# Chunks of 256 tokens as three passes of 256 columns, with both weight tiles shifted alike

## The chip, the cores and the metric

The kernel runs on one core of one Trainium2 chip. The metric is the device time of one execution in microseconds (us), as the median of several. Durations inside an execution come from one profiled execution, whose own time and span are given below.

## What is computed

One layer of a hybrid decoder trunk over 16 meta tokens and 256 sequence tokens (L = 272) with a model width of 2048. In the reference, cut to what matters here:

```
hn = rmsnorm(h_res, norm_g[l])                       # (272, 2048)
p = hn @ w_in[l]                                     # 176 blocks of 128 columns
glu_a, glu_b, conv_gate, q, k, v, ret_gate, merge_a, merge_b = ...  # slices of p
y_a = conformer_branch(...)      # glu, 31-tap conv, layernorm, * silu(conv_gate), @ conv_out
o = retention_chunkwise(q, k, v) # 8 heads
o = head_groupnorm(o, ...)
y_b = (o * silu(ret_gate)) @ ret_out[l]
merged = sigmoid(merge_a) * y_a + sigmoid(merge_b) * y_b
h_res = h_res + merged @ w_out[l]
return rmsnorm(h_res, final_norm_g)[:, 16:]
```

All inputs and outputs are float32. The output has 256 rows, so the parts that only scale or gate an output token (conv_gate, q, ret_gate, merge_a, merge_b) need the 256 sequence tokens alone, and the parts that feed the convolution or the keys and values need all 272.

## The kernel before

**Splitting.** TensorE multiplies in a float32r type. To keep float32 accuracy each operand is split into a high part and the rest (`split`, lines 52 to 54: a copy on ACT, a subtraction on DVE), and a product is the sum of three: high weights times high activations, high weights times low activations, low weights times high activations. The low-times-low product is left out.

**Chunks.** The program is one list `seq` of 240 weight chunks of 128 x 2048 floats (1 MB). Chunk i is loaded on the SP queue into `raw` (three buffers), split into a pair `whi` and `wlo` (three buffers each), and then used by TensorE. The engines run in the order in which the program issues to them; TensorE works chunk by chunk. 176 chunks are blocks of `w_in`, 32 of `ret_out`, 16 of `conv_out` and 16 of `w_out`.

**The activations.** `hn` holds the normalized tokens, transposed: 128 channels on the partitions, `[8, 2, 2, ROW]` behind it, that is block k mod 8, high or low, block k div 8, and a row of 288 floats of which 272 are used. `hn_row(k, low)` is a row of 272; `hn_wide(k)` is the high and the low row of block k without the 16 meta tokens, a pattern of 2 x 256.

**Two ways to multiply a chunk.** A chunk for all 272 tokens goes through `project` (lines 272 to 280): for each of 16 blocks k, high weights times the high row and high weights times the low row (lines 277 and 278), and then 16 times low weights times the high row (line 280). That is 48 matmuls of 272 columns into one PSUM row. A chunk for 256 tokens goes through `project_wide` (lines 282 to 289): high weights times both rows at once, 16 matmuls of 512 columns that fill two halves of a PSUM bank (line 289), and 16 matmuls of 256 columns with the low weights into the first half (line 288). The latter stand ahead of the last of the former. `halves` (lines 291 to 295) adds the two halves: ACT copies the second to SBUF (line 294), DVE adds the first (line 295). 96 chunks of `w_in` are of this kind (q, ret_gate, merge_b, conv_gate and merge_a), and the 16 of `conv_out`, whose activations are `fin["s"]`, written `s`.

**A third user of 256 columns** is `contract` (lines 297 to 304), for `ret_out`: three passes of 256 columns, high-high and high-low in turn (301, 302) and then low-high (304), with the tiles `zhi` and `zlo`. A chunk has 48 of these, and there are four chunks for each of the eight heads.

**Addresses.** Where the weights lie against the moving rows is set by hand in places. `halved` cuts a weight tile into two halves of 1024 floats, 1056 floats apart; the rows of blocks k and k + 8 in `hn` are 288 floats apart. Both distances are 128 bytes modulo 256, so that a block and its row keep one distance in both halves. The argument `first` of `stream` (16 for chunks of 256 tokens) shifts the low weights by 16 floats, 64 bytes, as the rows without the meta tokens start 16 floats further. The high weights are not shifted. By the addresses in the built program, the weight block that is loaded while a row streams lies 64 bytes (modulo 256) from that row in `project`, in `contract` and in the low passes of `project_wide`, and 0 bytes from it in most of the wide matmuls. At the step from block 7 to block 8 it is 128 bytes more, once in each pass over a halved tile.

The order of the 240 chunks: for each head sig_b and glu blocks, q and k, the four `ret_out` chunks of the head before, v, and the four ret_gate blocks; then 8 of merge_b, the last head's `ret_out`, 8 of merge_b, 16 of conv_gate, merge_a and `conv_out` in turn, and `w_out`.

Of the kernel before, what the change touches and what calls it, by code (L numbers as in the profile page):

```python
# [10 lines left out]
F32 = mybir.dt.float32  # L11
F32R = mybir.dt.float32r
AF = mybir.ActivationFunctionType
ALU = mybir.AluOpType
PSUM = bass.MemoryType.PSUM

P = 128
D = 2048
KT = D // P
# [20 lines left out]
def hybrid_kernel(ctx: ExitStack, tc, xt, xrow, xnat, par, fg, cs, dec, win, cout, rout, wout, out):  # L40
# [34 lines left out]
        return t[:, first:first + 2 * HALF_W].rearrange("p (h c) -> p h c", h=2)[:, :, 0:D // 2]  # L75

    def split_tiles(apart, first):
        hi = stage.tile([P, 2 * HALF_W], F32R, tag="whi", name="whi", bufs=SPLITS)
        lo = stage.tile([P, 2 * HALF_W + 64], F32R, tag="wlo", name="wlo", bufs=SPLITS)
        if not apart:  # L80
            return hi[:, 0:D], lo[:, first:first + D]
        return halved(hi), halved(lo, first)

    def block(w, k):
        return w[:, k * P:(k + 1) * P] if len(w.shape) == 2 else w[:, k // 8, k % 8 * P:(k % 8 + 1) * P]
# [193 lines left out]
        for k in ks:  # L279
            nc.tensor.matmul(acc[:, 0:L], lhsT=block(lo, k), rhs=hn_row(k, 0), start=False, stop=(k == KT - 1))  # L280

    def project_wide(acc, hi, lo, a):

        both = acc.rearrange("p (h t) -> p h t", h=2)
        for k in range(KT):
            if k == KT - 1:
                for j in range(KT):
                    nc.tensor.matmul(acc[:, 0:SEQ], lhsT=block(lo, j), rhs=a(j)[:, 0], start=False, stop=False)  # L288
            nc.tensor.matmul(both, lhsT=block(hi, k), rhs=a(k), start=(k == 0), stop=(k == KT - 1))  # L289

    def halves(acc, out):

        t = tmp.tile([P, SEQ], F32, tag="half", name="half")
        nc.scalar.copy(out=t, in_=acc[:, SEQ:])  # L294
        nc.vector.tensor_tensor(out=out, in0=acc[:, 0:SEQ], in1=t, op=ALU.add)

    def contract(acc, hi, lo, a_hi, a_lo, kts, col):

# [10 lines left out]
    def proj_chunk(blk, n, evac):  # L309
        def use(hi, lo, acc=None):  # L310
            if acc is not None:
                return lambda: evac(acc)
            acc = bank(misc if 4 <= seen[0] <= HELD else accp)
            seen[0] += 1
            if n == L:
                project(acc, hi, lo)
            else:
                project_wide(acc, hi, lo, hn_wide)
            return lambda: evac(acc)
        stream(win[blk], use, True, 0 if n == L else 16)  # L320

# [22 lines left out]
    def head(h):  # L344
# [20 lines left out]
        def rot(which, j, n):  # L365
            def f(acc):
                t = ret.tile([P, 2, n], F32, tag=f"rt{j}", name=f"rt{j}")
                s[which, j] = t
                if n == SEQ:
                    x = tmp.tile([P, SEQ], F32, tag="sg", name="sg")  # L370
                    halves(acc, x)
                    acc = x
                nc.vector.tensor_tensor(out=t, in0=acc[:, 0:n].unsqueeze(1).broadcast_to([P, 2, n]),
                                        in1=cs_sb[:, :, L - n:], op=ALU.mult)
                if j == 1:
                    t0, t1 = s[which, 0], t
                    r = ret.tile([P, 2, n], F32, tag=which + "r", name=which + "r")
                    nc.vector.tensor_tensor(out=r[:, 0], in0=t0[:, 0], in1=t1[:, 1], op=ALU.subtract)
                    nc.vector.tensor_tensor(out=r[:, 1], in0=t1[:, 0], in1=t0[:, 1], op=ALU.add)
                    hi = ret.tile([P, 2, n], F32R, tag=which + "hi", name=which + "hi")  # L380
                    lo = ret.tile([P, 2, n], F32R, tag=which + "lo", name=which + "lo")
                    split(r, hi, lo)
                    s[which] = (r, hi, lo)
            return f
# [8 lines left out]
        def gate(j):  # L393
            def f(acc):
                if j == 0:
                    s["g"] = ret.tile([P, 4 * SEQ + 16], F32, tag="gs", name="gs")[:, 0:4 * SEQ].rearrange(
                        "p (b t) -> p b t", b=4)
                g, t = s["g"][:, j], tmp.tile([P, SEQ], F32, tag="sg", name="sg")
                halves(acc, g)
                nc.vector.tensor_tensor(out=g, in0=g, in1=row[:, NMETA:], op=ALU.mult)  # L400
                nc.scalar.activation(out=t, in_=g, func=AF.Sigmoid)
                nc.vector.tensor_tensor(out=g, in0=g, in1=t, op=ALU.mult)
            return f
# [182 lines left out]
    fin = {}  # L586

    def sig_of(acc, t):
        halves(acc, t)
        nc.vector.tensor_tensor(out=t, in0=t, in1=row[:, NMETA:], op=ALU.mult)  # L590
        nc.scalar.activation(out=t, in_=t, func=AF.Sigmoid)

    def merge_b(d):
# [60 lines left out]
    def conv_gate(b):  # L654
        def f(acc):
            fp = fin["pool"]
            g = u_sb[b % 2][:, 0:SEQ]
            halves(acc, g)
            nc.vector.tensor_tensor(out=g, in0=g, in1=row[:, NMETA:], op=ALU.mult)
            t = tmp.tile([P, SEQ], F32, tag="sg", name="sg")  # L660
            nc.scalar.activation(out=t, in_=g, func=AF.Sigmoid)
            nc.vector.tensor_tensor(out=g, in0=g, in1=t, op=ALU.mult)
# [17 lines left out]
    def conv_out_use(d):  # L680
        def use(hi, lo):
# [1 line left out]
                fin["m"] = [pool.tile([P, NB, SEQ], F32R, tag=tag, name=f"m{i}")  # L683
                            for i, (pool, tag) in enumerate(((pers, "cm"), (fin["pool"], "m1")))]
            acc = bank(accp)
            project_wide(acc, hi, lo, lambda k: fin["s"][:, k])
            t = fin["ma", d]
            y = fin["pool"].tile([P, SEQ], F32, tag="lny", name="ya", bufs=2)
            halves(acc, y)
            nc.vector.tensor_tensor(out=t, in0=y, in1=t, op=ALU.mult)  # L690
            nc.vector.tensor_tensor(out=yb[:, d], in0=yb[:, d], in1=t, op=ALU.add)
            split(yb[:, d], fin["m"][0][:, d], fin["m"][1][:, d])
        return use
# [230 lines left out]
```

## Time and profile before

| what | value |
|---|---|
| median of 3 runs | 1415.52 us (1415.43 to 1416.01) |
| the profiled execution | 1416.04 us |
| its span, first to last instruction | 1414.3 us |
| PE busy with matmuls | 1404.7 us, 99% of the span |
| DVE, ACT busy | 1090.0 us, 691.4 us |
| bytes moved | 274.70 MB, 194 GB/s |

The span is what the trace shows; the execution's own time has 1.7 us around it. The profiled execution took 0.5 us more than the median. Matmuls overlap in the trace: one lasts longer than the time to the start of the next, so the pace is read from start to start, and the ends are modelled.

### The profile page before, as it was taken

Reading aid. Unit: us, or ns where it says so; the run is one execution under the profiler, and the core shown is the slowest. Engines: PE = TensorE matmul, PEld = TensorE weight load, DVE = VectorE, ACT = ScalarE, POOL = GpSimd, SP = SyncE. Lnnn points to the kernel's source line nnn. Section 1 sums busy time; section 2 is a strip of 40 time slices with the busy share of each in tenths; the row PEclk is TensorE's granted clock in tenths of the full one; section 3 lists DMA queues with packets and bytes.
Section 4 is the critical chain, followed back from the end, with each engine's and each line's share of the span. In section 5 each row is a group of like instructions: output and inputs, shape, how many; then the busy total and the mean of one; then the engine's idle time right before and its main releaser. Section 6 shows DMA issues by size and latency. Waiting matters only on the chain.

```text
span 1414.3 us, 23358 instructions
## 1 busy us (share of the span) xinstructions
PE 1404.7 (99%) x9648; PEld 1311.4 (93%) x9648; DVE 1090.0 (77%) x1513; ACT 691.4 (49%) x823; POOL 176.1 (12%) x317
## 2 busy tenths in 40 slices
PE   9999999999999999999999999999999999999997
PEld 9999999999999999999999999989988888888887
DVE  6799957986895797698689579976688876666553
ACT  6554635445544534544553454355356654444432
POOL 0032023003203201400320320032000000000000
PEclk9999999999999999999999999999999999999999
DMA  9665556556555655665555565566555555555752
GB/s 327 247 210 185 179 193 200 186 187 207 180 186 188 202 178 186 192 201 179 177 193 201 180 199 174 178 197 196 196 184 183 179 205 183 190 197 181 296 184 85
DMA packets 49467, 274.70 MB, mean 194 GB/s; under 512 B 9136, under 2 KB 9904, under 8 KB 18480
## 3 DMA queue, kind: packets, MB, share of 16 engines
q1 hardware_dynamic: 38352, 258.43, 53.1%
q0 software_dynamic: 9280, 8.93, 3.3%
q10 hardware_dynamic: 1728, 5.83, 1.2%
q8 instruction: 76, 1.25, 0.4%
q14 instruction: 31, 0.25, 0.0%
HBM read 262.15 MB, written 2.10 MB: 187 GB/s over the span
## 4 chain that ended last, share of the span: by engine, by line
PE 95%; DVE 2%; ACT 1%; DMA 1%; issue 1%; POOL 0%; POOLq 0%; DVEq 0%; ACTq 0%
PE ps L289 27%; PE ps L288 14%; PE ps L278 11%; PE ps L280 11%; PE ps L277 11%; PE ps L302 4%; PE ps L301 4%; PE ps L304 4%; PE ps L703 2%; PE ps L702 2%; PE ps L706 2%; DVE wlo L54 1%; DMA vy<-vx 0%; ACT whi L53 0%; PE ps L515 0%
## 5 line engine op out<-in xcount | busy, mean ns | idle before, releaser
L54 DVE TENSOR_TENSOR wlo<-raw,whi 128x2048 fp32r<-128x2048 f32 (+2 forms) x246 | 547.2, 2226 | 147.0 <-ACT whi L53 121.9
L53 ACT ACTIVATE whi<-raw 128x2048 fp32r<-128x2048 f32 (+2 forms) x246 | 459.6, 1870 | 270.0 <-PE ps L278 138.7
L289 PE MATMUL ps<-hn,whi 128*128 128x512 f32 x1536 | 374.7, 392 | 0.0
L289 PEld LDWEIGHTS ps<-hn,whi 128*128 128x128 f32 x1536 | 283.1, 188 | 55.7
L277 PE MATMUL ps<-hn,whi 128*128 128x272 f32 x1264 | 317.1, 287 | 0.0
L278 PE MATMUL ps<-hn,whi 128*128 128x272 f32 x1264 | 316.7, 287 | 0.0
L278 PEld LDWEIGHTS ps<-hn,whi 128*128 128x128 f32 x1264 | 238.2, 188 | 1.1
L277 PEld LDWEIGHTS ps<-hn,whi 128*128 128x128 f32 x1264 | 238.2, 188 | 0.3
L339 DVE SCALAR_TENSOR_TENSOR c_sb<-u,par_sb,c_sb 128x256 f32<-128x256 f32 x480 | 206.6, 476 | 1.5
L288 PEld LDWEIGHTS ps<-hn,wlo 128*128 128x128 f32 x1536 | 194.2, 189 | 7.6 <-DVE wlo L54 0.3
L288 PE MATMUL ps<-hn,wlo 128*128 128x256 f32 x1536 | 195.8, 280 | 0.0
L280 PE MATMUL ps<-hn,wlo 128*128 128x272 f32 x1264 | 171.1, 287 | 0.0
L280 PEld LDWEIGHTS ps<-hn,wlo 128*128 128x128 f32 x1264 | 162.8, 189 | 0.0
L294 ACT COPY half<-ps 128x256 f32<-128x256 f32 x112 | 41.5, 370 | 241.4 <-PE ps L289 241.1
L459 POOL DMA_DIRECT2D vy<-vx x128 | 73.6, 583 | 569.8 <-DVE xl L472 445.8
L301 PE MATMUL ps<-zhi,whi 128*128 128x256 f32 x512 | 123.0, 277 | 0.0
L302 PE MATMUL ps<-zlo,whi 128*128 128x256 f32 x512 | 123.0, 277 | 0.0
L301 PEld LDWEIGHTS ps<-zhi,whi 128*128 128x128 f32 x512 | 96.3, 188 | 0.0
L302 PEld LDWEIGHTS ps<-zlo,whi 128*128 128x128 f32 x512 | 96.2, 188 | 0.0
L459 POOL DMA_DIRECT2D oy<-ox x128 | 74.0, 585 | 42.5 <-DVE ox L535 27.2
L304 PE MATMUL ps<-zhi,wlo 128*128 128x256 f32 x512 | 79.1, 277 | 0.0
L304 PEld LDWEIGHTS ps<-zhi,wlo 128*128 128x128 f32 x512 | 67.8, 188 | 0.0
(176 smaller groups left out, 1182.2 us busy)
## 6 DMA issues: line engine op xcount, KB each, us to landing
raw<-in_win_dram SPq DMA_DIRECT2D x173, 1024.0 KB, 4.9
raw<-in_rout_dram SPq DMA_DIRECT2D x32, 1024.0 KB, 4.9
raw<-in_cout_dram SPq DMA_DIRECT2D x16, 1024.0 KB, 4.8
raw<-in_wout_dram SPq DMA_DIRECT2D x16, 1024.0 KB, 4.9
vy<-vx POOLq DMA_DIRECT2D x128, 32.0 KB, 3.0
oy<-ox POOLq DMA_DIRECT2D x128, 32.0 KB, 4.4
dec<-in_dec_dram ACTq DMA_DIRECT2D x8, 264.0 KB, 2.9
raw<-in_win_dram SPq DMA_DIRECT2D x8, 256.0 KB, 6.1
```

The costliest lines, as they stand in the source:

```text
L53: nc.scalar.activation(out=hi, in_=src, func=AF.Copy)
L54: nc.vector.tensor_tensor(out=lo, in0=src, in1=hi.bitcast(F32), op=ALU.subtract)
L277: nc.tensor.matmul(acc[:, 0:L], lhsT=w, rhs=hn_row(k, 0), start=(k == 0), stop=False)
L278: nc.tensor.matmul(acc[:, 0:L], lhsT=w, rhs=hn_row(k, 1), start=False, stop=False)
L280: nc.tensor.matmul(acc[:, 0:L], lhsT=block(lo, k), rhs=hn_row(k, 0), start=False, stop=(k == KT - 1))
L288: nc.tensor.matmul(acc[:, 0:SEQ], lhsT=block(lo, j), rhs=a(j)[:, 0], start=False, stop=False)
L289: nc.tensor.matmul(both, lhsT=block(hi, k), rhs=a(k), start=(k == 0), stop=(k == KT - 1))
L301: nc.tensor.matmul(acc, lhsT=hi[:, k, col], rhs=a_hi[:, k], start=(j == 0), stop=False)
L302: nc.tensor.matmul(acc, lhsT=hi[:, k, col], rhs=a_lo[:, k], start=False, stop=False)
L304: nc.tensor.matmul(acc, lhsT=lo[:, k, col], rhs=a_hi[:, k], start=False, stop=(j == n - 1))
L339: nc.vector.scalar_tensor_tensor(out=c, in0=u[:, t:t + SEQ], scalar=w, in1=c, op0=ALU.mult, op1=ALU.add)
L459: nc.gpsimd.dma_start(out=dst(q, a), in_=src(q, a))
```

## The change

Chunks of 256 tokens, and the `conv_out` chunks, go through a new function `project_seq` in place of `project_wide`. It makes the same three products as `project` does, in the same order, with 256 columns: 16 times a pair of high weights with the high row and with the low row, then 16 low-weight passes, all into the first half of the PSUM bank. `halves` is gone, and those who called it read PSUM directly. The high weights get the same shift `first` as the low ones, for which `whi` grows by 64 floats in each of three buffers. That moves every later tile by 768 bytes, a multiple of 256; the freed `half` tiles move the pools behind them by another multiple of 256.

```diff
     def split_tiles(apart, first):
-        hi = stage.tile([P, 2 * HALF_W], F32R, tag="whi", name="whi", bufs=SPLITS)
+        hi = stage.tile([P, 2 * HALF_W + 64], F32R, tag="whi", name="whi", bufs=SPLITS)
         lo = stage.tile([P, 2 * HALF_W + 64], F32R, tag="wlo", name="wlo", bufs=SPLITS)
         if not apart:
-            return hi[:, 0:D], lo[:, first:first + D]
-        return halved(hi), halved(lo, first)
+            return hi[:, first:first + D], lo[:, first:first + D]
+        return halved(hi, first), halved(lo, first)
...
-    def project_wide(acc, hi, lo, a):
-
-        both = acc.rearrange("p (h t) -> p h t", h=2)
+    def project_seq(acc, hi, lo, a):
+
+        o = acc[:, 0:SEQ]
         for k in range(KT):
-            if k == KT - 1:
-                for j in range(KT):
-                    nc.tensor.matmul(acc[:, 0:SEQ], lhsT=block(lo, j), rhs=a(j)[:, 0], start=False, stop=False)
-            nc.tensor.matmul(both, lhsT=block(hi, k), rhs=a(k), start=(k == 0), stop=(k == KT - 1))
-
-    def halves(acc, out):
-
-        t = tmp.tile([P, SEQ], F32, tag="half", name="half")
-        nc.scalar.copy(out=t, in_=acc[:, SEQ:])
-        nc.vector.tensor_tensor(out=out, in0=acc[:, 0:SEQ], in1=t, op=ALU.add)
+            nc.tensor.matmul(o, lhsT=block(hi, k), rhs=a(k)[:, 0], start=(k == 0), stop=False)
+            nc.tensor.matmul(o, lhsT=block(hi, k), rhs=a(k)[:, 1], start=False, stop=False)
+        for k in range(KT):
+            nc.tensor.matmul(o, lhsT=block(lo, k), rhs=a(k)[:, 0], start=False, stop=(k == KT - 1))
...
             else:
-                project_wide(acc, hi, lo, hn_wide)
+                project_seq(acc, hi, lo, hn_wide)
...
-                if n == SEQ:
-                    x = tmp.tile([P, SEQ], F32, tag="sg", name="sg")
-                    halves(acc, x)
-                    acc = x
...
-                halves(acc, g)
-                nc.vector.tensor_tensor(out=g, in0=g, in1=row[:, NMETA:], op=ALU.mult)
+                nc.vector.tensor_tensor(out=g, in0=acc[:, 0:SEQ], in1=row[:, NMETA:], op=ALU.mult)
...
-            project_wide(acc, hi, lo, lambda k: fin["s"][:, k])
+            project_seq(acc, hi, lo, lambda k: fin["s"][:, k])
             t = fin["ma", d]
-            y = fin["pool"].tile([P, SEQ], F32, tag="lny", name="ya", bufs=2)
-            halves(acc, y)
-            nc.vector.tensor_tensor(out=t, in0=y, in1=t, op=ALU.mult)
+            nc.vector.tensor_tensor(out=t, in0=acc[:, 0:SEQ], in1=t, op=ALU.mult)
```

`sig_of` and `conv_gate` are edited as the gate is (the hunk with `halves(acc, g)`).

On PE, the two q chunks of the first head stand like this before, between the small products that make the row of norms (line 266) and the next chunk of 272 tokens (line 277):

```order
L266 MATMUL ps<-ident,lhs 128x16
L289 MATMUL ps<-hn,whi 128x512 x15
L288 MATMUL ps<-hn,wlo 128x256 x16
L289 MATMUL ps<-hn,whi 128x512 x16
L288 MATMUL ps<-hn,wlo 128x256 x16
L289 MATMUL ps<-hn,whi 128x512
L277 MATMUL ps<-hn,whi 128x272
```

The same place after the change, at the end of the first chunk and the start of the second (lines 286 and 287 are the high weights with the high and the low row, line 289 the low weights):

```order
L286 MATMUL ps<-hn,whi 128x256
L287 MATMUL ps<-hn,whi 128x256
L286 MATMUL ps<-hn,whi 128x256
L287 MATMUL ps<-hn,whi 128x256
L289 MATMUL ps<-hn,wlo 128x256 x16
L286 MATMUL ps<-hn,whi 128x256
L287 MATMUL ps<-hn,whi 128x256
```

A chunk had 32 matmuls, 16 of them of 512 columns, and has 48 of 256; each matmul of both kinds has its own weight load.

On DVE, where merge_a and `conv_out` chunks alternate, an addition of two halves (line 295) stands before ahead of each product with what PSUM holds (line 590 for merge_a, 690 for `conv_out`):

```order
L295 TENSOR_TENSOR sg<-ps,half 128x256
L590 TENSOR_TENSOR sg<-sg,row 128x256
L54 TENSOR_TENSOR wlo<-raw,whi 128x2048
L295 TENSOR_TENSOR ya<-ps,half 128x256
L690 TENSOR_TENSOR sg<-ya,sg 128x256
```

At the same place after the change the products (now lines 578 and 675) read PSUM (`ps`) themselves, and the split of the next weights stands between them as before:

```order
L578 TENSOR_TENSOR sg<-ps,row 128x256
L54 TENSOR_TENSOR wlo<-raw,whi 128x2048
L675 TENSOR_TENSOR sg<-ps,sg 128x256
L54 TENSOR_TENSOR wlo<-raw,whi 128x2x1024
L676 TENSOR_TENSOR yb<-yb,sg 128x256
```

One DVE addition and one ACT copy of each of the 112 chunks are gone; the splits (line 54) keep their places.

## Rows read from the trace of the kernel before

**Rows 1.** The page: span, PE's busy time, granted TensorE clock in 40 slices.
```profile
span 1414.3 us, 23358 instructions
PE 1404.7 (99%) x9648; PEld 1311.4 (93%) x9648; DVE 1090.0 (77%) x1513; ACT 691.4 (49%) x823; POOL 176.1 (12%) x317
PEclk9999999999999999999999999999999999999999
```

**Rows 2.** The page: the chain that ended last, by engine.
```profile
PE 95%; DVE 2%; ACT 1%; DMA 1%; issue 1%; POOL 0%; POOLq 0%; DVEq 0%; ACTq 0%
```

**Rows 3.** Waits of PE: total us, times, longest us.
```profile
PE ps L160 <- DVE zeros L150: 1.1, 1, 1.1
PE ps L636 <- DVE cs_sb L628: 0.5, 1, 0.5
PE ps L278 <- DVE hn L208: 0.2, 1, 0.2
```

**Rows 4.** PE groups by line and shape: count | busy us, mean ns | idle.
```profile
L289 PE MATMUL ps<-hn,whi 128*128 128x512 f32 x1536 | 374.7, 392 | 0.0
...
L289 PE MATMUL ps<-s,whi 128*128 128x512 f32 x256 | 63.5, 391 | 0.0
```

**Rows 5.** Chain in order of time, late chunks of 256 tokens: start us, us.
```profile
1058.20 3.67 PE ps L289 x16
...
1146.95 3.67 PE ps L289 x16
```

**Rows 6.** Timeline of PE, an hn chunk and a conv_out chunk: start us, us.
```profile
1235.72 3.59 PE L289 MATMUL ps<-hn,whi 128*128 128x512 f32 x15
1239.15 2.04 PE L288 MATMUL ps<-hn,wlo 128*128 128x256 f32 x16
1241.03 0.40 PE L289 MATMUL ps<-hn,whi 128*128 128x512 f32 x1
1241.27 3.59 PE L289 MATMUL ps<-s,whi 128*128 128x512 f32 x15
...
1246.81 3.59 PE L289 MATMUL ps<-hn,whi 128*128 128x512 f32 x15
```

**Rows 7.** Timeline of PE, four ret_out chunks behind a chunk of 272 columns.
```profile
628.58 0.28 PE L301 MATMUL ps<-zhi,whi 128*128 128x256 f32 x1
...
629.05 0.28 PE L301 MATMUL ps<-zhi,whi 128*128 128x256 f32 x1
...
650.36 0.28 PE L277 MATMUL ps<-hn,whi 128*128 128x272 f32 x1
```

**Rows 8.** Timeline of PE, the last head's ret_out chunks, behind a wide chunk.
```profile
983.32 0.40 PE L289 MATMUL ps<-hn,whi 128*128 128x512 f32 x1
983.56 0.28 PE L301 MATMUL ps<-zhi,whi 128*128 128x256 f32 x1
...
1005.58 0.28 PE L302 MATMUL ps<-zlo,whi 128*128 128x256 f32 x1
```

**Rows 9.** One line's instructions by stretch: duration ns min/median/max, first, last start.
```profile
L304 PE MATMUL ps<-zhi,wlo x64: 276/276/276, 629.5 to 650.2; 128*128 128x256 f32 x64
L304 PE MATMUL ps<-zhi,wlo x63: 281/281/281, 984.5 to 1005.9; 128*128 128x256 f32 x63
L288 PE MATMUL ps<-hn,wlo x8: 280/281/284, 1026.7 to 1027.5; 128*128 128x256 f32 x8
L288 PE MATMUL ps<-hn,wlo x10: 276/280/284, 1027.4 to 1028.5; 128*128 128x256 f32 x10
```

**Rows 10.** Timeline of PE, one chunk of 272 columns.
```profile
599.60 0.29 PE L277 MATMUL ps<-hn,whi 128*128 128x272 f32 x1
...
605.55 0.40 PE L289 MATMUL ps<-hn,whi 128*128 128x512 f32 x1
```

**Rows 11.** ACT and DVE groups of the sum of halves, and ACT's wait.
```profile
L294 ACT COPY half<-ps 128x256 f32<-128x256 f32 x112 | 41.5, 370 | 241.4 <-PE ps L289 241.1
L295 DVE TENSOR_TENSOR sg<-ps,half 128x256 f32<-128x256 f32 x40 | 16.8, 421 | 22.3 <-ACT half L294 22.3
ACT half L294 <- PE ps L289: 241.1, 85, 5.2
```

More of the change, by code (lines that the diff above doesn't have):

```diff
@@ L588, in sig_of @@
     def sig_of(acc, t):
-        halves(acc, t)
-        nc.vector.tensor_tensor(out=t, in0=t, in1=row[:, NMETA:], op=ALU.mult)
+        nc.vector.tensor_tensor(out=t, in0=acc[:, 0:SEQ], in1=row[:, NMETA:], op=ALU.mult)
         nc.scalar.activation(out=t, in_=t, func=AF.Sigmoid)
@@ L657, in f @@
             g = u_sb[b % 2][:, 0:SEQ]
-            halves(acc, g)
-            nc.vector.tensor_tensor(out=g, in0=g, in1=row[:, NMETA:], op=ALU.mult)
+            nc.vector.tensor_tensor(out=g, in0=acc[:, 0:SEQ], in1=row[:, NMETA:], op=ALU.mult)
             t = tmp.tile([P, SEQ], F32, tag="sg", name="sg")
```

## The prediction

> **What bounds the kernel.** I read the page first: PE is busy for 1404.7 of 1414.3 us, and its granted clock is full in every slice, the higher of its two levels, 2.4 GHz [rows 1]. The chain that ended last is 95% PE [rows 2]. Then the waits of PE: the three that the view lists come to 1.8 us [rows 3]. So nothing but PE's own pace is worth much here: an edit that takes work from DVE or ACT buys nothing, and one that changes the time from one matmul to the next buys all of it. The reader should distrust the durations (392 ns for a wide matmul, [rows 4]), which overlap, and divide the time between two starts by the number of matmuls between them.
>
> **What a chunk of 256 tokens costs now.** There are 1536/16 = 96 on `hn` and 256/16 = 16 on `s` [rows 4]. In the late stretch, where they follow each other, 16 chunks take 1146.95 - 1058.20 = 88.75 us, 5.547 us each [rows 5]. One `hn` chunk beside one `s` chunk: 1241.27 - 1235.72 = 5.55 and 1246.81 - 1241.27 = 5.54 us [rows 6]. Each streams 16 x 512 + 16 x 256 = 12,288 columns, 0.4514 ns a column. The changed chunk streams 48 x 256 = 12,288 columns as well. The change takes away no PE work; it can only change the pace at which columns go by.
>
> **What pace 48 matmuls of 256 columns can have.** The old trace shows this product three times.
>
> First, `contract`: three passes of 256 columns, with the same distance of 64 bytes (modulo 256) between the loaded block and the streamed row that the change sets. Behind a chunk of 272 columns its 192 matmuls take 650.36 - 628.58 = 21.78 us, 113.4 ns each [rows 7], and all 64 of the low passes there last 276 ns [rows 9]. In the last head, behind a wide chunk, 187 matmuls take 1005.58 - 983.56 = 22.02 us, 117.75 ns each [rows 8], and all 63 low passes listed last 281 ns [rows 9]. Same code, same tiles, same distance: two paces, each of which holds for 22 us. I call them free and held. What differs is what went before.
>
> Second, the low passes of a wide `hn` chunk. Line 288 takes 1241.03 - 1239.15 = 1.88 us for 16, 117.5 ns each [rows 6]. Here the durations tell the story: the first eight last 280 to 284 ns, so they are held, and in the view of the later ones a matmul of 276 ns appears [rows 9]. The 284 is the step from block 7 to block 8, where the distance is 128 bytes off for one load; I call it a switch. So held passes behind a switch come free.
>
> Third, `project`, which has the very order of the new function but 272 columns: 605.55 - 599.60 = 5.95 us a chunk [rows 10], 124.0 ns a matmul, 0.4557 ns a column.
>
> For 12,288 columns these give 5.443 us (free throughout), 5.652 (held throughout) and 5.600 (at the pace of `project`), against 5.547 now. The ends lie on both sides, so the switches decide. A changed `hn` chunk has four: one in the high passes, one at the turn from high to low, one in the low passes, one into the next chunk. An `s` chunk has none inside, its rows and weights being unbroken.
>
> **What a switch costs a free stream.** No row shows a free stream of 256 columns go through one. From below: the switch's own 284 - 276 = 8 ns [rows 9]. From above: it may drop the stream to the held pace until the next switch. The nearest row is the entry of `contract` behind the 272-column chunk: the first four matmuls take 629.05 - 628.58 = 0.47 us where free ones take 0.454 [rows 7], so the stream comes in disturbed, pays 16 ns (to within 10, as starts are shown in hundredths of a us) and is free. A changed chunk resembles this more than the wide one, since neither has 512-column matmuls. I take 16 ns a switch, 64 ns a chunk.
>
> **The sum.** `hn` chunks: 5.443 + 0.064 = 5.507, 0.040 less than 5.547, times 96: -3.8 us. `s` chunks: 5.443 + 0.016 for the entry = 5.459, 0.081 less than 5.54, times 16: -1.3 us. The last head's `contract` would follow a chunk of 256-column passes, not a wide one, and come free: 192 x (117.75 - 113.4) ns = -0.8 us. Together -5.9 us.
>
> **What counts for nothing.** The sums of halves were 112 copies of 370 ns on ACT and 112 additions of some 421 ns on DVE [rows 11]. ACT stood waiting for PE's end of chunk before 85 of those copies, 241.1 us in all [rows 11], and PE waits for neither engine beyond 1.8 us [rows 3]: PE's own length covers them, before and after. Without that cover they would cost 112 x 0.79 = 89 us. The product that now reads PSUM waits for the same last matmul as the copy did; behind it on DVE stands the split of a chunk that PE needs a chunk or more later. The load queue gets no new entry. Each chunk has 48 weight loads where it had 32; `contract` and `project` have 48 too, and `contract` shows 113.4 ns for load and matmul together [rows 7], so more loads alone cost nothing. The tiles all move by multiples of 256 bytes, which leaves the other products' distances, modulo 256, as they were.
>
> **A rule on the other side.** The same instruction on the same tiles lasts 276 or 281 ns [rows 9], and with these the pace goes by 4%. The Trainium skill's page SBUF — State Buffer, section Who interferes with whom, gives PE two independent read ports, one for the moving operand and one for weight loads, and says that only the pair of ports shared by VectorE and GpSimd is contended. By that rule no distance between weights and rows matters, equal columns take equal time, and the sum is 0, 1416.0 us. The trace doesn't agree: something that outlasts one matmul slows the same stream by 4%.
>
> **The rivals.**
> - *A switch drops a free stream to the held pace, and the next one frees it.* For it: the first eight low passes of a wide chunk stay held from their entry to the switch [rows 9]; `project`, which has these switches, runs at 0.4557 ns a column [rows 10]. Against: held was seen only behind 512-column matmuls [rows 8, 9]. Of the stretches between switches (16, 16, 8 and 8 matmuls) one of 16 and one of 8 are held: 24 x 4.35 = 104 ns, with two entries of 16 ns and four switches of 8 ns, 5.611 us a chunk, +0.064 x 96 = +6.1 us, the other terms about nil: 1422. It ends slower than now from the point at which a switch costs (5.547 - 5.443)/4 = 26 ns.
> - *Held nearly throughout.* 5.652 + 0.016 = 5.668, +0.121 x 96 = +11.6, `s` +1.8: 1429. Against it: a switch is what released line 288.
> - *The switches cost about 26 ns,* so the chunk stays at 5.55 and only the `s` chunks and the last head gain: about 1414. For it: the entry's 16 ns and the 284's 8 ns may add.
> - *No disturbance at all:* -0.104 x 96 - 0.097 x 16 - 0.8 = -12.3 us: 1403.
> - *The pace goes by columns whatever the distance,* the rule above: 1415.5.
>
> **The numbers.** Against the profiled execution's 1416.04 us the sum gives 1410.1; it ran 0.5 us above the median of 1415.52, so 1409.6 us for the median. A measurement of this kernel can tell about 0.2% (2.8 us) from no change. Chances: free with cheap switches, 1403 to 1412, 0.48; switches at about 26 ns, 0.15; the rule, 0.05; dropped and freed in turn, 0.22; held, 0.10. So faster 0.48, same 0.20, slower 0.32. The range runs from no disturbance at all, 1403, to just beyond the first rival, 1423; the likeliest case alone has 1403 to 1412.
>
> **What would show it.** In the changed kernel's timeline a late `hn` chunk should take 5.48 to 5.53 us and an `s` chunk 5.44 to 5.46; most matmuls of the new lines should last 276 ns with a few of 280 to 284 behind each switch; the last head's `contract` should last 276 throughout; chunks of 272 columns should keep 5.95 us and PE's waits stay under 3 us. If the medians of the new lines are 280 or more, the step on the switches is wrong and the time is 1420 or above. If `s` chunks are held though they have no switch, the entry is what I have misread. A wait of PE for a split or for a PSUM bank, which I cost at nothing, would show as a gap between chunks.

## The result and the profile after

The change makes the kernel slower: 1425.8 us median of 4 runs (1425.67 to 1426.01) against 1415.6 us for the kernel before on the same chip (1415.43 to 1416.01), a ratio of 1.0072 with a 95% interval of 1.0054 to 1.0089. The forecast was 1409.6 us, its range 1403 to 1423: wrong in sign, and the time lies outside the range.

First the page, to see whether something other than PE's pace moved: the span, PE's row of busy time and the chain by engine. They answer to [rows 1, 2].

```profile
span 1424.0 us, 26691 instructions
PE 1414.6 (99%) x11440; PEld 1396.4 (98%) x11440; DVE 1044.9 (73%) x1401; ACT 667.9 (47%) x711; POOL 176.5 (12%) x317
PE 99%; DVE 0%; issue 0%; ACT 0%; POOLq 0%; POOL 0%
```

DVE and ACT are busy for 45.1 and 23.5 us less than before, and that bought nothing. PE is busy for 9.9 us more, and the span is 9.7 us longer. PE's waits, the whole view, answer to [rows 3] and stay at 1.8 us:

```profile
PE ps L160 <- DVE zeros L150: 1.1, 1, 1.1
PE ps L624 <- DVE cs_sb L616: 0.7, 1, 0.7
```

So the loss is pace, and the late chunks show how much. The chain in order of time (start us, us; line 289 is a chunk's low passes) answers to [rows 5]:

```profile
1065.93 1.89 PE ps L289 x16
...
1155.64 1.89 PE ps L289 x16
```

The two rows are 16 chunks apart: 89.71/16 = 5.607 us a chunk on `hn`, 5.547 before. PE's timeline (start us, us) has the first matmuls of an `hn` chunk, of the `conv_out` chunk on `s` behind it, and of the next one, and answers to [rows 6]:

```profile
1201.57 0.28 PE L286 MATMUL ps<-hn,whi 128*128 128x256 f32 x1
...
1207.16 0.28 PE L286 MATMUL ps<-s,whi 128*128 128x256 f32 x1
...
1212.62 0.28 PE L286 MATMUL ps<-hn,whi 128*128 128x256 f32 x1
```

The `s` chunk takes 5.46 us (5.54 before), as forecast. The `hn` chunk beside it takes 5.59. Where an `hn` chunk loses is seen in one line's instructions by stretch (duration in ns min/median/max, first and last start), here of one chunk that starts at 1037.7, and of the `s` chunk above:

```profile
L286 PE MATMUL ps<-hn,whi x3: 279/280/280, 1037.7 to 1038.2; 128*128 128x256 f32 x3
L286 PE MATMUL ps<-hn,whi x4: 276/276/276, 1038.4 to 1039.1; 128*128 128x256 f32 x4
L286 PE MATMUL ps<-hn,whi x8: 281/281/281, 1039.5 to 1041.2; 128*128 128x256 f32 x8
L289 PE MATMUL ps<-hn,wlo x16: 278/281/284, 1041.4 to 1043.2; 128*128 128x256 f32 x16
...
L286 PE MATMUL ps<-s,whi x16: 276/276/280, 1207.2 to 1210.6; 128*128 128x256 f32 x16
```

A 276 is a matmul at the free pace, one of 278 or more at the held pace, as in [rows 9]. The chunk starts held: the switch at its entry frees it, but only behind some five matmuls (280 ns). The rest of the first half of its high passes is free. The switch from block 7 to block 8, at 1039.4, drops it to the held pace, and the remaining two thirds of the chunk, all its low passes among them, stay there, across the turn from high to low and the switch in the low passes. That makes some 37 of 48 matmuls held. The `s` chunk has no switch inside; it too starts held (280), and behind its entry it stays free.

The place where the prediction expected no loss is `ret_out`, whose code the change doesn't touch. Its low passes over the whole run, by line, answer to [rows 9]:

```profile
L298 PE MATMUL ps<-zhi,wlo x512: 281/281/283, 153.8 to 1014.6; 128*128 128x256 f32 x171
```

The timeline has the first matmul of one head's four chunks and the first behind them, as [rows 7] have:

```profile
633.65 0.28 PE L295 MATMUL ps<-zhi,whi 128*128 128x256 f32 x1
...
656.26 0.29 PE L277 MATMUL ps<-hn,whi 128*128 128x272 f32 x1
```

Those four chunks took 21.78 us before; now they take 656.26 - 633.65 = 22.61, the held pace (22.61/192 = 117.8 ns a matmul). Before, only the last head's were held [rows 8]; now all eight heads' are.

The sum, an estimate that gives every chunk of a kind the length read above: 80 `hn` chunks 5.607 - 5.547 = 0.060 us longer, +4.8; the 16 beside an `s` chunk 5.59 - 5.55, +0.6; 16 `s` chunks 0.08 us shorter, -1.3; `ret_out` of seven heads 0.83 us longer, +5.8. Together +9.9 us, where the spans differ by 9.7.

### The profile page after: what moved, and what is told of

Its sections match the earlier page's. It is cut to its first block, busy times and chain, and to the rows that moved or that the text cites. A ratio compares the mean times of both kernels' runs of the same rounds, so it can differ in the third digit from the quotient of the medians.

```text
span 1424.0 us, 26691 instructions
## 1 busy us (share of the span) xinstructions
PE 1414.6 (99%) x11440; PEld 1396.4 (98%) x11440; DVE 1044.9 (73%) x1401; ACT 667.9 (47%) x711; POOL 176.5 (12%) x317
## 4 chain that ended last, share of the span: by engine, by line
PE 99%; DVE 0%; issue 0%; ACT 0%; POOLq 0%; POOL 0%
PE ps L289 15%; PE ps L286 14%; PE ps L287 14%; PE ps L278 11%; PE ps L277 11%; PE ps L280 11%; PE ps L295 4%; PE ps L298 4%; PE ps L296 4%; PE ps L688 2%; PE ps L691 2%; PE ps L687 2%; PE ps L505 0%; PE ps L504 0%; PE ps L503 0%; PE ps L160 0%
## 5 line engine op out<-in xcount | busy, mean ns | idle before, releaser
L286 PE MATMUL ps<-hn,whi 128*128 128x256 f32 x1536 | 362.0, 279 | 0.0
L287 PE MATMUL ps<-hn,whi 128*128 128x256 f32 x1536 | 361.4, 279 | 0.0
L287 PEld LDWEIGHTS ps<-hn,whi 128*128 128x128 f32 x1536 | 289.7, 189 | 0.1
L286 PEld LDWEIGHTS ps<-hn,whi 128*128 128x128 f32 x1536 | 289.5, 189 | 0.1
L277 PEld LDWEIGHTS ps<-hn,whi 128*128 128x128 f32 x1264 | 238.5, 189 | 0.4
L278 PEld LDWEIGHTS ps<-hn,whi 128*128 128x128 f32 x1264 | 238.2, 188 | 0.4
L289 PEld LDWEIGHTS ps<-hn,wlo 128*128 128x128 f32 x1536 | 187.5, 188 | 0.0
L280 PEld LDWEIGHTS ps<-hn,wlo 128*128 128x128 f32 x1264 | 162.9, 189 | 0.0
L296 PE MATMUL ps<-zlo,whi 128*128 128x256 f32 x512 | 126.4, 281 | 0.0
L295 PE MATMUL ps<-zhi,whi 128*128 128x256 f32 x512 | 126.4, 281 | 0.0
```

The costliest lines, as they stand in the source:

```text
L277: nc.tensor.matmul(acc[:, 0:L], lhsT=w, rhs=hn_row(k, 0), start=(k == 0), stop=False)
L278: nc.tensor.matmul(acc[:, 0:L], lhsT=w, rhs=hn_row(k, 1), start=False, stop=False)
L286: nc.tensor.matmul(o, lhsT=block(hi, k), rhs=a(k)[:, 0], start=(k == 0), stop=False)
L287: nc.tensor.matmul(o, lhsT=block(hi, k), rhs=a(k)[:, 1], start=False, stop=False)
L289: nc.tensor.matmul(o, lhsT=block(lo, k), rhs=a(k)[:, 0], start=False, stop=(k == KT - 1))
L295: nc.tensor.matmul(acc, lhsT=hi[:, k, col], rhs=a_hi[:, k], start=(j == 0), stop=False)
```

## The experiments

Theory: the time between two matmuls is set by how the load of the next block stands to the row that streams meanwhile. With both at one distance it is 113.3 ns (free) or 117.8 ns (held), and the stream keeps whichever it has. A load off the distance, a switch, drops a free stream to held; on a held one it may free it. Rivals: 48 weight loads in a chunk, where there were 32, are what costs; or the columns alone set the pace, whatever the distance. The eleven kernels ran in four groups; times are compared with the kernel before in the same group (1416.3 to 1416.5 us), by which the changed kernel stands 10.2 us above it. Some executions of the kernel before run up to 1424 us, which widens a few intervals; of these there is no profile.

### No switches at all (unbroken)

From the changed kernel: rows and halves of the weights without a gap, so that no load inside a chunk is off the distance. Some small tiles move to make room.

```
-ROW = 288
-HALF_W = 1024 + 32
+ROW = 320
+HALF_W = 1024
```

> The changed kernel with the rows of hn 320 floats apart and the weight halves 1024 floats apart, so that no load inside a chunk, of 256 or of 272 tokens, is off the distance of 64 bytes. Theory (a pace, free or held, is inherited from one matmul to the next and only a load off the distance changes it): an hn chunk no longer goes at one pace for a part and at the other for the rest; either about 5.45 us throughout, some 1405 us in all if ret_out is free too, or about 5.65 us throughout, some 1430 us. Rival (48 weight loads a chunk cost more than 32, whatever their distance): hn chunks stay at 5.61 us and the time at 1425.8.

Measured: 1418.99 us median of 10 runs, one of them 1408.84; ratio 1.0006 (0.9986 to 1.0025). The profiled execution shows both paces, each without a mixture. One line by stretch, early and late:

```profile
L283 PE MATMUL ps<-hn,whi x48: 276/276/276, 86.5 to 100.8; 128*128 128x256 f32 x48
L283 PE MATMUL ps<-hn,whi x481: 281/281/281, 1059.8 to 1308.5; 128*128 128x256 f32 x161
```

The chain of the late chunks (start us, us):

```profile
1071.48 1.89 PE ps L286 x16
...
1156.28 1.89 PE ps L286 x16
```

The heads' 54 chunks of 256 tokens from 81.0 to 980 us are free throughout; the first head's two q chunks, ahead of them, are held. The late ones, 15 of them in 84.80 us, take 5.653 us each and are held for 250 us, `s` chunks included. Same instructions, same distances, same number of loads: the rival that counts loads falls, since 48 loads and matmuls go by in 5.44 us. So does the rival that the columns alone set the pace: equal columns take 5.44 or 5.65 us here. The early chunks give 54 x (5.547 - 5.440) = 5.8 us, and the late held ones and `ret_out`, held too, give it back. An even distance by itself is thus worth nothing here: it keeps the held pace as well as the free one.

### A switch in each s chunk (s_broken)

From the changed kernel, the `conv_out` weights and the rows of `s` get the gap that those of `hn` have (the new layout of `s` is not printed here).

```
...
-        stream(cout[d], conv_out_use(d), first=16)
+        stream(cout[d], conv_out_use(d), True, 16)
```

> The changed kernel, but the conv_out chunks get halved weight tiles and their activations a gap of 128 bytes behind block 7, as the hn chunks have. Theory: the 16 conv_out chunks go from 5.46 us to 5.58 to 5.61 us, with part of their matmuls held, and the time rises by 2.0 to 2.4 us to about 1428. Rival (conv_out chunks are faster than hn chunks for what they read or how they are emptied): they stay at 5.46 us, 1425.8.

Measured: 1428.74 us (1428.40 to 1429.21, 5 runs), ratio 1.0075 (1.0051 to 1.0099), 12.4 us above the kernel before, 2.2 more than the changed one. The chain runs evenly now, `hn` and `s` chunks alike, 61.68/11 = 5.607 us:

```profile
1161.42 1.89 PE ps L289 x16
...
1223.10 1.89 PE ps L289 x16
```

The gap alone takes an `s` chunk from 5.46 to 5.607 us, the `hn` chunk's time. This is the price of the switches by themselves.

### Wide q chunks again (q_wide)

From the changed kernel, the two q chunks of each head, which come two 272-column chunks ahead of `ret_out`, are made wide as before, with their sum of halves (the line that asks for it is printed; `project_wide` and the sum come back as they were).

```
...
-                proj_chunk(base + 2 * h + j, n, rot(which, j, n))
+                proj_chunk(base + 2 * h + j, n, rot(which, j, n), n == SEQ)
```

> The changed kernel, but the 16 q chunks go back to the wide product with unshifted high weights and a sum of halves, at the changed kernel's addresses. Theory (ret_out inherits its pace through the k chunks from the q chunks): the ret_out chunks of heads 0 to 6 are free again, 276 ns a matmul in place of 281, 5.9 us less, and 16 q chunks of 5.55 instead of 5.61 take 1.0 us more off: about 1418.9. Rival (the move of the tiles by 768 bytes holds ret_out): ret_out stays at 281 ns, about 1424.8.

Measured: 1422.96 us (1419.93 to 1428.20, 10 runs), ratio 1.0031 (1.0008 to 1.0054). The time missed its number; the lowest run is 1.0 us above it. The profiled execution, 1425.79 us, holds a PE wait of 4.2 us in the last head's `attend`; whether the other long ones do is not shown. The point was `ret_out`, by line and shape (count, busy us, mean ns, idle):

```profile
L304 PE MATMUL ps<-zhi,whi 128*128 128x256 f32 x512 | 123.0, 277 | 0.0
```

The mean is 277 again, as it was before the change; it is 281 in the changed kernel. So `ret_out`'s pace came from the q chunks, through 12 us of other chunks whose own length stays 5.95 us. These are the two k chunks, of 272 columns: in this layout they hand on a held pace.

### Only conv_out in three passes (s_only2)

From the kernel before, `conv_out` alone is changed, with both its weight tiles shifted (not printed).

```
...
-            project_wide(acc, hi, lo, lambda k: fin["s"][:, k])
+            project_seq(acc, hi, lo, lambda k: fin["s"][:, k])
```

> The kernel before, with only the conv_out chunks as three passes of 256 columns and both their weight tiles shifted. Theory: conv_out chunks 5.46 us in place of 5.54, the rest as before: 1.3 us less, about 1414.2. Rival (more loads cost time): conv_out chunks 5.6 us or more, about 1416.7.

Measured: 1418.01 us (1417.44 to 1418.53, 10 runs), ratio 0.9996 (0.9978 to 1.0013). The theory's 1414.2 was missed; the rival's 5.6 us or more a chunk and 1416.7 us are nearer, but not for its reason, as 48 loads went by in 5.44 us above. The chunks stand between wide ones, and they are held:

```profile
L295 PE MATMUL ps<-s,whi x224: 281/281/281, 1175.4 to 1319.0; 128*128 128x256 f32 x112
```

The same chunk that is free in the changed kernel (276, above) is held here, behind a wide chunk. I had taken the pace of a chunk without switches for its own. I now read it as inherited from the wide chunk; whether that chunk's own pace or the load at the border does it was not separated.

### The high weights not shifted (hi_unshifted)

From the changed kernel, the high weights lie where they lay before, 0 bytes from the rows.

```
-            return hi[:, first:first + D], lo[:, first:first + D]
-        return halved(hi, first), halved(lo, first)
+            return hi[:, 0:D], lo[:, first:first + D]
+        return halved(hi), halved(lo, first)
```

> The changed kernel without the shift of the high weights, so that in the high passes the loaded block lies 0 bytes, modulo 256, from the streamed row. Theory (the distance sets the pace): matmuls of 256 columns at distance 0 took 120 ns in the output product, so a chunk takes 32 x 120 + 16 x 117 ns = 5.71 us and the time is 1425.8 + 96 x 0.10 + 16 x 0.25 = about 1439. Rival (the distance does not matter, only the number of passes): 1425.8.

Measured: 1430.14 us (1430.00 to 1430.51, 4 runs), ratio 1.0087 (1.0063 to 1.0112). High passes are slower than held ones:

```profile
L286 PE MATMUL ps<-hn,whi 128*128 128x256 f32 x1536 | 371.6, 283 | 0.0
...
L295 PE MATMUL ps<-zhi,whi 128*128 128x256 f32 x512 | 122.5, 276 | 0.0
```

The shift of the high weights, a line of the diff, is worth having. The time is 9 us below the expected 1439. Of these, `ret_out`, which came free (276), makes 8 x 0.83 = 6.6 us that the expectation did not have; a late `hn` chunk takes 5.68 us where 5.71 was expected, which makes about the rest. Why `ret_out` came free here is open.

### One late chunk of 272 columns (release)

From the kernel with unbroken rows: the second `conv_gate` chunk is made for all 272 tokens, as k chunks are, and 256 of them are used.

```
...
-        proj_chunk(G0 + b, SEQ, conv_gate(b))
+        proj_chunk(G0 + b, SEQ, conv_gate(b), b == 1)
```

> The unbroken layout, and one conv_gate chunk behind the last stall of PE (the second one) computed for all 272 tokens through the 48 matmuls of 272 columns, of which the 256 are used. Theory (a stall leaves the stream held, a chunk of 272 columns ahead frees it, and unbroken chunks then stay free): the 46 chunks behind it go from 5.65 to 5.44 us, 9.8 us less, the chunk itself 0.3 more: 1419.0 - 9.5 = about 1409.5. Rival (late in the program the pace is held by what else the chip does there): no change, 1419.3.

Measured: 1409.46 us (1409.29 to 1410.76, 6 runs), ratio 0.9941 (0.9919 to 0.9963). The late chain has 15 chunks in 81.60 us, 5.440 each:

```profile
1067.02 1.81 PE ps L286 x16
...
1148.62 1.81 PE ps L286 x16
```

The high passes by stretch, ahead of that chunk and behind it:

```profile
L283 PE MATMUL ps<-hn,whi x79: 280/281/281, 1022.0 to 1049.3; 128*128 128x256 f32 x79
L283 PE MATMUL ps<-hn,whi x459: 276/276/276, 1069.8 to 1300.5; 128*128 128x256 f32 x153
```

More work, and 9.5 us less than without it. But the profile does not show the 272-column chunk (1057.3 to 1063.2) doing it: the chunk just ahead of it is free already, behind the small products of the layernorm at 1051.4, which had left the stream held in the profile without it. The times say more: all six executions lie at 1409.3 to 1410.8 us, where of the 18 of the two unbroken kernels without the late chunk only two do as well (1408.84 and 1408.76 us). The last experiment separates the two in another place.

### The same, with ret_out kept free (release_ret)

In addition, k goes ahead of q in every head, so that `ret_out` follows a 256-column chunk directly, and `ret_out`'s weights and `z` tiles move by 64 bytes, so that the load at the border is on the distance too.

```
...
-        for which, base, n in (("q", Q0, SEQ), ("k", K0, L))[::1 if h else -1]:
+        for which, base, n in (("q", Q0, SEQ), ("k", K0, L))[::-1]:
...
-            stream(rout[4 * h + g], use)
+            stream(rout[4 * h + g], use, first=16)
```

> The same, and the ret_out chunks made part of one unbroken stream: k ahead of q in every head, the weights of ret_out and its activations shifted by 64 bytes. Theory: the 32 ret_out chunks enter free and stay so, 113.4 instead of 117.8 ns a matmul, 6.8 us less than release: about 1402.7. Rival (ret_out has its own reason to be held): no change against release.

Measured: 1402.17 us (1401.84 to 1402.69, 5 runs), ratio 0.989 (0.9868 to 0.9911): 14.2 us below the kernel before in its group, where the changed kernel was 10.2 above. Its `ret_out` is free in all heads:

```profile
L292 PE MATMUL ps<-zhi,whi x512: 276/276/276, 151.7 to 995.7; 128*128 128x256 f32 x171
```

That is worth 1409.46 - 1402.17 = 7.3 us, where eight heads at 0.83 us would give 6.6. The order of q and k and the 64 bytes were changed together, so which of them does it is not shown. This version beats both kernels.

### Half the switches (lo_back)

From the changed kernel, low passes start at block 8, where the high ones ended, and end at block 7. Two of a chunk's four switches go.

```
-        for k in range(KT):
+        for k in list(range(8, KT)) + list(range(8)):
```

> The changed kernel with the low passes starting at block 8, so that a chunk has two loads off the distance (in the high passes behind block 7, and in the low passes behind block 15) instead of four. Theory (a step from the first half to the second holds a free stream, a step back frees a held one): 24 of 48 matmuls held where the changed kernel has 32, 5.57 us a chunk, 96 x 0.035 = 3.4 us less, 1422.5 if ret_out stays held, 1416.5 if it comes free. Rival (each such load costs time by itself, about 9 ns): 2 x 9 x 96 = 1.7 us less, with the share of held matmuls as it was.

Measured: 1420.82 us (1420.57 to 1421.59, 7 runs), ratio 1.0032 (1.002 to 1.0043). The chain of the late chunks:

```profile
1069.79 1.85 PE ps L289 x16
...
1153.39 1.85 PE ps L289 x16
```

The low passes of `ret_out` in the first seven heads, and the last ones of a q chunk ahead of it:

```profile
L298 PE MATMUL ps<-zhi,wlo x448: 275/276/277, 153.8 to 889.7; 128*128 128x256 f32 x150
...
L289 PE MATMUL ps<-hn,wlo x3: 277/277/278, 259.9 to 260.1; 128*128 128x256 f32 x3
```

83.60/15 = 5.573 us a chunk, as expected, and no more than 0.034 gained for half of the switches. `ret_out` comes free again, though the q chunks are still made of 256 columns: the q chunk ends free (277). With `ret_out` free the expectation had 1416.5 us; the `s` chunks, held now (281 on average), take 3 of the missing 4.3 us.

### Three passes over each half (by_halves)

From the changed kernel, all three products of blocks 0 to 7 go first, then those of 8 to 15: two switches less, in another order. The matmuls inside the loops stay as they are and are left out here.

```
-        for k in range(KT):
...
-        for k in range(KT):
...
+        for g in (range(8), range(8, KT)):
+            for k in g:
...
+            for k in g:
...
```

> The changed kernel with all three passes over blocks 0 to 7 first and then over blocks 8 to 15; the two loads off the distance lie behind the 24th and the 48th matmul. Theory: as lo_back, 24 of 48 held, the first 24 free but for six behind the entry, 5.57 us a chunk, 1422.5 or 1416.5. Rival as there.

Measured: 1423.99 us (1423.69 to 1424.34, 4 runs), ratio 1.0054 (1.0039 to 1.0069), with one PE wait of 1.5 us for a split of weights. The chain of the late chunks:

```profile
1072.08 0.94 PE ps L290 x8
...
1155.68 0.94 PE ps L290 x8
```

The group of `ret_out`'s first line (count, busy us, mean ns, idle), and the last passes of a q chunk ahead of it:

```profile
L296 PE MATMUL ps<-zhi,whi 128*128 128x256 f32 x512 | 126.4, 281 | 0.0
...
L290 PE MATMUL ps<-hn,wlo x8: 281/281/283, 261.8 to 262.6; 128*128 128x256 f32 x8
```

Again 83.60/15 = 5.573 us a chunk: with two switches in either order the chunk takes the same. `ret_out` is held, unlike in the kernel with low passes from block 8, and here the q chunk ends held (281). In this layout the pace at which q ends thus goes with that of `ret_out`, in the changed kernel too (both at 281); the kernel with unshifted high weights is an exception, where q ends at 281 and `ret_out` is free.

### Another distance (dist_192)

From the changed kernel, both weights are shifted by 192 bytes, not 64.

```
-        stream(win[blk], use, True, 0 if n == L else 16)
+        stream(win[blk], use, True, 0 if n == L else 48)
...
-        stream(cout[d], conv_out_use(d), first=16)
+        stream(cout[d], conv_out_use(d), first=48)
```

> The changed kernel with both weight tiles shifted by 48 floats instead of 16 in chunks of 256 tokens, so that the distance is 192 bytes and a step between halves makes it 64 once. Theory (the distance decides whether loads and rows meet): the paces differ from 113.4 and 117.8 ns; a chunk at more than 5.61 us if 192 is a worse distance, as the 122 ns of a single load at 192 suggest, up to 48 x 122 = 5.86 us and 1425.8 + 112 x 0.25 = 1454. Rival (any constant distance does): 1425.8.

Measured: 1432.66 us (1432.24 to 1432.80, 4 runs), ratio 1.0114 (1.0099 to 1.0129). The `s` chunks, which have no switch, and the first half of the high passes (and one more, behind the switch) of the chunk behind the last head's `ret_out`, which comes free here:

```profile
L286 PE MATMUL ps<-s,whi x256: 278/279/281, 1165.7 to 1333.2; 128*128 128x256 f32 x128
...
L286 PE MATMUL ps<-hn,whi x9: 276/276/279, 1016.5 to 1018.3; 128*128 128x256 f32 x9
```

The `s` chunks go at the held pace (278 to 281 ns; the late chunks of both kinds take 5.65 us), although the changed kernel's are free in the same place. The side was as expected, the size far below the upper bound. But the distance of 192 bytes does not itself hold a stream: the second line is a stretch at this distance that came in free and stayed free for its 16 high passes, until the switch (the 279). The same two paces exist here; the difference is that no switch in the late chunks frees the stream any more.

### A chunk of 272 columns behind held ones (release_early)

From the kernel with unbroken rows: the chunk made for 272 tokens is the first one behind the last head's `ret_out`, which ends held.

```
...
-        proj_chunk(MB0 + d, SEQ, merge_b(d))
+        proj_chunk(MB0 + d, SEQ, merge_b(d), d == EARLY)
```

> The kernel with unbroken rows, with one other chunk made for all 272 tokens: not a late one, but the first merge_b chunk behind the last head's ret_out, which comes held out of it (5.65 us a chunk there, with 256 columns). Theory (a chunk of 272 columns gives back the free pace, whatever comes in): the two 256-column chunks behind it and ahead of the first layernorm products take 5.44 us each, their durations 276 ns, where they took 5.65. Rival (it gives nothing back; that the late stretch was free in the kernel with the late 272-column chunk came from the small layernorm products ahead of it, behind which its profile shows 276 ns already): they stay at 5.65 us and 281 ns. The late stretch, behind the small products, is left to those in both: 1409 if they leave it free, about 1419 if held, less 0.1 us for the two chunks and the longer one together, so the time tells little and the durations of the two chunks decide.

Measured: 1419.4 us (1408.76 to 1421.05, 8 runs), ratio 1.0007 (0.9982 to 1.0032). The rows that decide, by line and stretch: `ret_out`'s low passes ahead of the chunk, the two chunks behind it, and those behind the first small products, at 1020:

```profile
L295 PE MATMUL ps<-zhi,wlo x63: 280/281/282, 981.6 to 1003.0; 128*128 128x256 f32 x63
...
L283 PE MATMUL ps<-hn,whi x32: 275/277/281, 1009.2 to 1018.0; 128*128 128x256 f32 x32
L283 PE MATMUL ps<-hn,whi x64: 280/281/468, 1020.3 to 1041.0; 128*128 128x256 f32 x64
```

The same stretch in the kernel with unbroken rows, without that chunk:

```profile
L283 PE MATMUL ps<-hn,whi x48: 280/281/281, 1003.3 to 1018.1; 128*128 128x256 f32 x48
```

The chain from the 272-column chunk on:

```profile
1007.34 1.98 PE ps L277 x16
1012.96 1.81 PE ps L286 x16
1018.40 1.81 PE ps L286 x16
1024.41 1.89 PE ps L286 x16
1030.07 1.88 PE ps L286 x16
```

Held in, free out: the two chunks behind the 272 columns go at 276 or 277 ns, and 1018.40 - 1012.96 = 5.44 us, where without it those chunks were held. So the chunk does give back the free pace, the theory's case. Whether its longer rows do it or the loads at its two borders, where the shift of the weights changes, was not separated. Nor does it hold for every such chunk: in the changed kernel, whose chunks have switches, the first ret_gate chunk of a head stands directly behind one and is held (here at 561.7 us):

```profile
L286 PE MATMUL ps<-hn,whi x16: 279/281/281, 561.7 to 565.2; 128*128 128x256 f32 x16
```

The two small products at 1020.05 take the free pace away again, and by the times the late stream stays held in seven of eight executions. This also says what the late chunk in `release` is for: it stands behind the last of those products.

## Why the prediction was wrong

- *What bounds the kernel, and what counts for nothing:* right. PE's busy time and the span rose together by 9.9 and 9.7 us, PE's waits stayed at 1.8 us, and the 69 us taken from DVE and ACT are not seen in the time.
- *Equal columns, so only the pace can change:* right. Chunks of 272 columns, untouched, kept their 5.95 us.
- *`s` chunks at 5.459 us:* right, 5.46, and -1.3 us, with some luck: the 5.440 of a free chunk and five held matmuls at the entry (some 22 ns, not 16). The reason given, that they have no switch, is borne out by the kernel that gives them one (5.607). But it is half of the reason: something at their entry must free the stream too, which happens behind an `hn` chunk of the changed kernel and not in the kernel with `conv_out` alone.
- *"I take 16 ns a switch":* this is the step that failed first. The price was read off an entry behind a 272-column chunk, a disturbance that the stream recovers from at once. A switch inside 256-column passes does not cost a sum of nanoseconds: it drops the stream to the held pace, about 4.5 ns a matmul, until something frees it. The `hn` chunk takes 5.607 us, not 5.507: 0.100 us on 96 chunks, 9 us. The first rival, given 0.22, had the drop right and came near the price (5.611), but by luck: it let the next switch free the stream, 24 held matmuls and 64 ns for entries and switches. Measured, neither the turn nor the switch in the low passes frees it, and (5.607 - 5.440)/0.0045 = 37 matmuls are held. That a switch released line 288 before [rows 9] did not carry over.
- *"The last head's `contract` would ... come free", and "the other terms about nil":* this failed next, and in every case that I listed, the rivals too. `ret_out` became held in seven heads, +5.8 us, and did not become free in the last. I had treated its pace as a thing of its own code and the chunk directly ahead. [Rows 7, 8] showed two paces for one code, and I asked what the last head would follow, not what the other seven would. With this term the first rival would have been 1428; with it and the `s` chunks' -1.3, about 1426.5 against the measured 1425.8.
- *The rule that distance does not matter,* as the prediction drew it from two independent read ports for PE (the Trainium skill's page SBUF — State Buffer, section Who interferes with whom): the runs disagree. Moving the weights from 64 to 192 bytes raises the ratio from 1.0072 to 1.0114, and moving rows, weights and `z` tiles, with k ahead of q and one chunk that streams more columns, brings it to 0.989.

Shown by experiment: switches cost the `hn` chunk its time; q chunks decide `ret_out`'s pace in the changed kernel; 48 loads do not cost anything by themselves; in the unbroken layout a chunk of 272 columns gave back the free pace in the place where it was tried. Still open: why a switch frees a held stream in some places (behind the last low pass of an `hn` chunk, and in the kernel with low passes from block 8) and not in others (at the turn from high to low, and in the low passes of the changed kernel); and what keeps the pace. By their times, one of ten and one of eight executions of the unbroken kernels come out of the small layernorm products free; what decides that was not tried.

## What to carry to other kernels

When one instruction has two durations in one trace, the pace is a state that is handed on: before pricing a change by the chunk it touches, ask which state it leaves behind, and list every later stretch that inherits it. Make the distance between the loaded weights and the streamed rows the same for every load, at the borders between products too; a single load off it cost up to 4% of what followed here, until something freed the stream. An even distance alone was not enough: it keeps whichever pace comes in. And if a stretch has lost the pace, a cheap break in the right place, behind the last disturbance, can be worth more than the work it adds.

## What the runs showed that I had not expected

- Matmuls of 256 columns go at 113.3, 117.8 or, 0 bytes from the rows in the kernel with unshifted high weights, about 119.4 ns (3.82 us for 32 high passes), at the same granted clock; the first two with the same code and addresses, for up to 250 us.
- A larger chunk made the kernel faster: 272 columns in place of 256 in one chunk of 112, 1418.99 to 1409.46 us. The chunks that always had 272 columns gain a little from unbroken rows as well, 5.92 us (61.49 to 67.41 in that kernel's profile) in place of 5.95.
- In the profiled execution of the kernel with wide q chunks PE stood still for 4.2 us, and the granted clock was lower only after it had resumed. The windows (stretch, its us, PE's busy us and count, granted clock, share of the DMA engines and GB/s among the columns):

```profile
944.90:949.40 4.50, 0.31 (x2) 0.00 (x0) 1.86 (x4) 4.38 (x6) 0.00 (x0) 1.00 0.00 2
949.40:952.20 2.80, 2.77 (x8) 2.18 (x9) 2.80 (x4) 2.61 (x3) 0.00 (x0) 0.68 0.23 29
952.20:954.00 1.80, 1.80 (x11) 1.79 (x10) 1.80 (x2) 0.04 (x1) 0.00 (x0) 0.55 0.78 291
954.00:956.00 2.00, 2.00 (x20) 2.00 (x19) 1.55 (x5) 0.00 (x0) 0.27 (x1) 1.00 0.94 336
```

  PE is idle for nearly all of the first window at a granted clock of 1.00; in the next two it works at 0.68 and 0.55 of the higher level, 2.4 GHz, the last near the lower one, 1.2 GHz, and in the fourth the clock is back. By these rows I estimate that beside itself the wait costs 2.80 x 0.32 + 1.80 x 0.45 = 1.7 us of full clock.
